# Attention weights split behind the exponentials and partly by transfers; a fifth pair of hidden tiles and another order of norms in the first feed-forward stage

## The chip, the cores and the metric

The kernel runs on one core of one Trainium2 chip. The metric is the device time of one execution, in microseconds. The kernel before takes 1312.35 us (median of three runs, 1311.97 to 1312.97).

Engines: PE (TensorE) multiplies matrices, DVE (VectorE) and ACT (ScalarE) work element by element and move matmul results from PSUM to SBUF, POOL (GpSimd) does small vector work and issues some DMAs, SP (SyncE) issues most DMAs.

## The reference, cut to what matters

A trunk of two layers over 512 tokens of width 1024: a Mamba-2 layer, then attention with a compressed key and value, each followed by a feed-forward network and by layer norms of a weighted residual.

```python
def trunk(x):
    mix = ssd_mixer(x, ...)
    h = layer_norm(DN_ALPHA * x + mix, ln_mix_g[0], ln_mix_b[0])
    h = layer_norm(DN_ALPHA * h + conv_ffn(h, ...), ln_ffn_g[0], ln_ffn_b[0])
    k_nope, k_rope, v = mla_shared_kv(h, ...)
    mix = mla_attention(h, ..., k_nope, k_rope, v)
    h = layer_norm(DN_ALPHA * h + mix, ln_mix_g[1], ln_mix_b[1])
    return layer_norm(DN_ALPHA * h + conv_ffn(h, ...), ln_ffn_g[1], ln_ffn_b[1])

def conv_ffn(h, up, conv_w, conv_b, down):
    u = causal_depthwise_conv(h @ up, conv_w, conv_b)
    g, val = jnp.split(u, 2, axis=-1)
    return (jax.nn.silu(g) * val) @ down

def attend(h):
    q = rms_norm(h @ q_down) @ q_up
    scores = q_nope @ k_nope.T + q_rope @ k_rope.T
    return softmax(where(causal, scores * scale, -inf)) @ v
```

The feed-forward network has 2816 hidden channels, 22 tiles of 128. Attention has 8 heads of 128, with 64 more rotary dimensions.

## The kernel before, in words

All matmuls run in a reduced-precision form of float32, and each operand is split into a high and a low half so that three matmuls (high by high, high by low, low by high) give back the precision. The activations' halves are made when a result leaves PSUM: ACT writes the high half as a cast, DVE subtracts it from the result and writes the low half. Weights go through `WStream`. It loads them in order into staging tiles `wst`, and `_split` (L76) makes two tiles of each: ACT casts `wh` (L96), DVE subtracts `wl` (L97). Six such pairs of buffers exist; `ahead(i, most)` splits as far as they and its bound allow, and `retire` gives a pair back after its last matmul.

The order of each engine's instructions is fixed when the program is built. A scheduler follows the order of the code with its own priorities, and `tc.issue_after` holds work back behind a named instruction. SP's loads are in the order of `load` calls.

The feed-forward stage (`ffn`, L420) works channel tile by channel tile: two weights, gate and value, with 24 matmuls each (`mm_a`, L159), then convolution, gate and product on ACT and DVE (`finish`). The down projection uses a form in which two hidden tiles (a pair) and two halves of the output share seven products in place of eight; `down_pairs` (L361) runs the products a11, s1, s2 with s4, s3, a12, a22 on the banks X, Y and Z. RP0 and RP1 (L288) give the pairs of each round, in parts of two or one that share a weight tile. In the first feed-forward stage the first round has five pairs (tiles 0 to 9), the second four (10 to 17); tiles 18 to 21 are plain. Sums of weight tiles that the pairs need are gathered in `rs` by loads on POOL's queue that add to what stands there (L52). After the rounds, the last part (L526) runs over the four token tiles: the plain tiles' down product, `piece`, in two halves of 12 matmuls, then `add_mix` (L185) to the residual with its sum, mean (L189), squares (L194, on ACT), variance and reciprocal deviation (L203, L204, on POOL), and the norm itself in `ln_a` (L210) and `ln_b` (L215). `transpose_h` (L267) then transposes the tile on PE and writes both halves of `ht`, which the next stage multiplies.

Attention (`mla`) begins with `down(i)` for the four token tiles, 48 matmuls each against six weights dw0 to dw5, each followed by `down_t` on the tile before. The transposes of tiles 0 and 1 stand inside the last part of the feed-forward stage, those of 2 and 3 behind down(0) and down(1). The head loop (L1352) then runs, for head h: the queries and keys of head h+1 (`qk`, evicted as qT and kT in L1235 and L1236; `qk_rope` for every second head), the value product of head h-1 (`pv`, evicted as oT in L1307 and L1308), the transposes of head h's probabilities (`ptrans`, L1288), and the scores of head h+1 (`scores`: matmul L1265, mask, maximum, exponential L1277 on ACT, scaling L1279 on DVE into E). Two calls of `ws.ahead(n[0], most=1)` per head split one weight each: hw1 to hw7 (640 wide, one per head) and the output weights ow0 to ow7 (1024 wide).

## Time and profile before

| | |
|---|---|
| median of three runs | 1312.35 us (1311.97 to 1312.97) |
| the profiled execution | 1311.7 us |
| its span | 1310.0 us |
| PE busy | 1299.5 us (99%) |
| DVE busy | 1020.6 us (78%) |
| ACT busy | 636.0 us (49%) |
| POOL busy | 93.1 us (7%) |
| mean granted PE clock | 0.998 of full speed, the 2.4 GHz level |

The span is the time from the first to the last instruction; the execution's own time has 1.7 us around it. Busy time is the time in which an engine has an instruction under way. A group of matmuls in the chain of work overlaps from one to the next, so the length of a group over its count gives the pitch of one, and the duration of a single matmul is longer than that.

### The profile page before, as it was taken

How to read it: one execution, taken by the hardware profiler on the slowest of the kernel's cores; microseconds unless marked ns; L12 is line 12 of the kernel's file. 1: busy time of each engine (PE TensorE's matmuls, PEld its weight loads, DVE VectorE, ACT ScalarE, POOL GpSimd, SP SyncE). 2: the span in 40 equal slices, each digit the busy share in tenths (PEclk: the TensorE clock that was granted, in tenths of full speed). 3: DMA queues.
4: the chain of work that ended last, by engine and by line, in shares of the span. 5: the costliest groups of instructions: out<-in, count | busy, mean ns of one | idle time of the engine just before them, and what ended most of it. 6: DMA issues, size and time to landing. Idle time of an engine off the chain costs nothing.

```text
span 1310.0 us, 17422 instructions
## 1 busy us (share of the span) xinstructions
PE 1299.5 (99%) x6666; PEld 1098.9 (84%) x6666; DVE 1020.6 (78%) x1581; ACT 636.0 (49%) x1029; POOL 93.1 (7%) x96
## 2 busy tenths in 40 slices
PE   9999999999999999999999999999999999999997
PEld 8888888888888988888888899888898888888886
DVE  7888888797798868866766876898587686667587
ACT  6765555455453544444443434665254444444341
POOL 0111011011011001100000012000100010000000
PEclk9999999999999999999999999999999999999999
DMA  8423322313410433352311822121144227323251
GB/s 297 179 113 129 113 88 90 132 58 133 161 65 10 171 129 81 80 207 98 123 58 31 254 81 62 71 107 49 35 149 135 79 35 213 130 97 105 41 161 65
DMA packets 49779, 144.59 MB, mean 110 GB/s; under 512 B 5312, under 2 KB 6336, under 8 KB 48416
## 3 DMA queue, kind: packets, MB, share of 16 engines
q1 hardware_dynamic: 44480, 133.57, 28.8%
q0 software_dynamic: 5072, 9.77, 4.4%
q8 instruction: 52, 0.85, 0.3%
q14 instruction: 31, 0.25, 0.1%
q10 hardware_dynamic: 144, 0.15, 0.0%
HBM read 141.30 MB, written 2.16 MB: 110 GB/s over the span
## 4 chain that ended last, share of the span: by engine, by line
PE 95%; DVE 4%; ACT 1%; issue 0%; DVEq 0%; ACTq 0%
PE ps L159 57%; PE ps L165 10%; PE ps L167 10%; PE ps L166 10%; PE ps L803 1%; PE ps L915 1%; PE ps L811 1%; PE ps L274 1%; PE ps L792 1%; PE ps L742 1%; PE ps L1265 1%; DVE wl L97 1%; DVE PT L1291 1%; PE ps L770 1%; DVE E L1279 0%; DVE smx L1275 0%
## 5 line engine op out<-in xcount | busy, mean ns | idle before, releaser
L159 PE MATMUL ps<-ht,wh 128*128 128x512 f32 (+1 forms) x2256 | 517.0, 379 | 0.0
L159 PEld LDWEIGHTS ps<-ht,wh 128*128 128x128 f32 x2256 | 408.1, 188 | 79.7 <-issue 1.4
L97 DVE TENSOR_TENSOR wl<-wst,wh 128x1024 fp32r<-128x1024 f32 (+3 forms) x222 | 256.3, 1169 | 44.2 <-ACT wh L96 43.3
L96 ACT CAST wh<-wst 128x1024 fp32r<-128x1024 f32 (+3 forms) x222 | 218.8, 995 | 114.3 <-PE ps L167 62.3
L159 PE MATMUL ps<-ht,wl 128*128 128x512 f32 (+1 forms) x1128 | 266.6, 378 | 0.0
L159 PEld LDWEIGHTS ps<-ht,wl 128*128 128x128 f32 x1128 | 205.2, 188 | 39.6
L328 DVE SCALAR_TENSOR_TENSOR acc<-ps,cw,acc 128x511 f32<-128x511 f32 x88 | 65.7, 747 | 80.0 <-ACT acc L327 80.0
L165 PE MATMUL ps<-wh,gt 128*128 128x512 f32 (+1 forms) x320 | 123.7, 387 | 0.0
L167 PE MATMUL ps<-wh,gt 128*128 128x512 f32 (+1 forms) x320 | 123.6, 386 | 0.0
L166 PE MATMUL ps<-wl,gt 128*128 128x512 f32 (+1 forms) x320 | 123.6, 386 | 0.0
L340 ACT CAST gt<-acc 128x512 fp32r<-128x512 f32 (+1 forms) x80 | 44.0, 571 | 102.0 <-DVE acc L333 99.3
L657 DVE SCALAR_TENSOR_TENSOR cv<-ps,cw,cv 128x511 f32<-128x511 f32 (+2 forms) x96 | 71.3, 746 | 26.8 <-ACT cv L655 25.9
L327 ACT ACTIVATE acc<-ps,cw 128x512 f32<-128x512 f32 x88 | 68.3, 776 | 29.5 <-PE ps L159 29.4
L167 PEld LDWEIGHTS ps<-wh,gt 128*128 128x128 f32 x320 | 60.1, 188 | 12.3
L332 ACT ACTIVATE acc<-acc 128x512 f32<-128x512 f32 x44 | 27.8, 632 | 87.6 <-DVE acc L329 87.5
L165 PEld LDWEIGHTS ps<-wh,gt 128*128 128x128 f32 x320 | 60.1, 188 | 12.1
L166 PEld LDWEIGHTS ps<-wl,gt 128*128 128x128 f32 x320 | 60.1, 188 | 12.1
L329 DVE SCALAR_TENSOR_TENSOR acc<-ps,cw,acc 128x510 f32<-128x510 f32 x88 | 65.8, 748 | 2.5
L52 POOL DMA_DIRECT2D rs<-in_down_dram x24 | 25.4, 1058 | 572.7 <-DVE wl L97 572.7
L96 ACT CAST wh<-rs 128x1024 fp32r<-128x1024 f32 (+1 forms) x48 | 39.9, 834 | 46.4 <-DVE rs L88 27.1
L341 DVE TENSOR_TENSOR gt<-acc,gt 128x512 fp32r<-128x512 f32 (+1 forms) x80 | 48.8, 627 | 13.5 <-ACT gt L340 13.5
L387 DVE SCALAR_TENSOR_TENSOR h<-h,ps 128x512 f32<-128x512 f32 x56 | 37.6, 686 | 26.0 <-PE ps L167 26.0
(242 smaller groups left out, 1744.7 us busy)
## 6 DMA issues: line engine op xcount, KB each, us to landing
wst<-in_up_dram SPq DMA_DIRECT2D x88, 512.0 KB, 3.5
wst<-in_xbc_dram SPq DMA_DIRECT2D x32, 512.0 KB, 6.0
wst<-in_down_dram SPq DMA_DIRECT2D x26, 512.0 KB, 5.5
W<-cumd SPq DMA_DIRECT2D x8, 1024.0 KB, 4.6
wst<-in_sow_dram SPq DMA_DIRECT2D x16, 512.0 KB, 3.6
wst<-in_zw_dram SPq DMA_DIRECT2D x14, 512.0 KB, 6.1
rs<-in_down_dram POOLq DMA_DIRECT2D x12, 512.0 KB, 6.9
wst<-in_down_dram SPq DMA_DIRECT2D x18, 256.0 KB, 2.6
```

The lines of the kernel that those rows point to most:

```text
L96: nc.scalar.copy(h[:, :f], s[:, :f])
L97: nc.vector.tensor_tensor(l[:, :f], s[:, :f], h[:, :f], op=ALU.subtract)
L159: nc.tensor.matmul(out, w[:, k, :], xts[k][:, x, ts], start=first and p == 0 and k == 0, stop=last and p == 2 and k == nk - 1, skip_group_ ...
L165: nc.tensor.matmul(out, xt[:, 0, tsl], wh, start=start, stop=False, skip_group_check=True)
L166: nc.tensor.matmul(out, xt[:, 0, tsl], wl, start=False, stop=False, skip_group_check=True)
L167: nc.tensor.matmul(out, xt[:, 1, tsl], wh, start=False, stop=stop, skip_group_check=True)
L327: nc.scalar.activation(a, b, AF.Identity, bias=cw[:, ch, 3:4], scale=cw[:, ch, 2:3])
L328: nc.vector.scalar_tensor_tensor(a[:, 1:], b[:, :SEQ - 1], cw[:, ch, 1:2], a[:, 1:], op0=ALU.mult, op1=ALU.add)
L329: nc.vector.scalar_tensor_tensor(a[:, 2:], b[:, :SEQ - 2], cw[:, ch, 0:1], a[:, 2:], op0=ALU.mult, op1=ALU.add)
L340: k.nc.scalar.copy(dst[:, 0, :], src)
L341: k.nc.vector.tensor_tensor(dst[:, 1, :], src, dst[:, 0, :], op=ALU.subtract)
L657: nc.vector.scalar_tensor_tensor(t[:, d:], b[:, :SEQ - d], cw[:, ch, 3 - d:4 - d], t[:, d:], op0=ALU.mult, op1=ALU.add)
```

## The change

In `_split` a new kind "d" makes the low half without DVE: ACT writes the negative of the weight, rounded, into `wl`, and a DMA on POOL's queue adds the staged weight to it. Seventeen weights have this kind: dw0 to dw5, hw1 to hw7 and ow0 to ow3. In the head loop one call for up to two weights, behind the last exponential and scaling of the next head's scores, stands in place of the two calls for one each.

In the first feed-forward stage the second round has five pairs, tiles 10 to 19. Tiles 20 and 21, the plain ones, are computed behind the first product a11 (`late`); the banks Y and Z are taken later, and the norm's parameters are loaded behind s2 and s4. The last part has 6 matmuls per half tile in place of 12. Its loop is written out anew for this stage: tile 0 is transposed behind tile 2's second half, tile 1's squares and norm come behind that, and tiles 1, 2 and 3 are transposed inside down(0), down(1) and down(2), after 33 of 48 matmuls (MID).

```diff
@@ WStream._split
         nc.scalar.copy(h[:, :f], s[:, :f])
-        nc.vector.tensor_tensor(l[:, :f], s[:, :f], h[:, :f], op=ALU.subtract)
+        if kind == "d":
+            nc.scalar.activation(l[:, :f], s[:, :f], AF.Copy, scale=-1.0)
+            nc.gpsimd.dma_start(l[:, :f], s[:, :f], accum_op=ALU.add)
+        else:
+            nc.vector.tensor_tensor(l[:, :f], s[:, :f], h[:, :f], op=ALU.subtract)
@@ rounds
-RP0 = ((2, 2, 1), (2, 1, 1))
+RP0 = ((2, 2, 1), (2, 2, 1))
+NGT = 18
...
-    return r0, r0 + 2 * sum(rp[1])
+    r1 = r0 + 2 * sum(rp[1])
+    return r0, r1, min(HT, r1 + NGT - 3 * sum(rp[1]) - (sum(rp[1]) + 1) // 2)
@@ down_pairs
         product(X, "a11", p, n + p, True, True)
     n += ni
     ahead(n, add(X, 0, 0, 1))
+    n = late(n)
+    Y = new_banks()
     for p in range(ni):
         product(Y, "s1", p, n + p, True, True)
     n += ni
     ahead(n, add(Y, 1, 1, 1))
-    between()
     for p in range(ni):
         product(X, "s2", p, n + 2 * p, False, True)
         product(Y, "s4", p, n + 2 * p + 1, False, True)
     n += 2 * ni
+    between()
+    Z = new_banks()
@@ ffn, the last part of the first stage
+            for i in range(NT):
+                added = half(i, 0)
+                if i == 1:
+                    with tc.issue_after(added.ins):
+                        ln_b(0, 0)
+                        ln_b(0, 1)
+                half(i, 1)
+                if i == NT - 1:
+                    ws.ahead(n + 2 * nw, la)
+                if i == 2:
+                    a, d = k.transpose_h(0)
+                    with tc.issue_after(a.ins), tc.issue_after(d.ins):
+                        squares(1)
+                        norm_a(1)
+                        for f in range(2):
+                            ln_b(1, f)
+                k.ln_mean(i)
+                if i != 1:
+                    squares(i)
+                    norm_a(i)
+                if i == NT - 1:
+                    for j in (2, NT - 1):
+                        for f in range(2):
+                            ln_b(j, f)
...
-        k.pend = [lambda: k.transpose_h(NT - 2), lambda: k.transpose_h(NT - 1)]
+        k.pend = [lambda i=i: k.transpose_h(i) for i in range(1, NT)]
@@ mla
+                if mid and c == MID:
+                    mid()
...
-            down(i)
-            if k.pend:
-                k.pend.pop(0)()
+            down(i, k.pend.pop(0) if k.pend else None)
@@ mla, the head loop
-                ends = qk(h + 1)
-                a, d = qk_rope(h + 1) or ends
-                with tc.issue_after(a.ins), tc.issue_after(d.ins):
-                    ws.ahead(n[0], most=1)
+                qk(h + 1)
+                qk_rope(h + 1)
...
-            a, d = ptrans(h)
+            ptrans(h)
             if h + 1 < AH:
+
+                a, d = scores(h + 1)
                 with tc.issue_after(a.ins), tc.issue_after(d.ins):
-                    ws.ahead(n[0], most=1)
-            if h + 1 < AH:
-                scores(h + 1)
+                    ws.ahead(n[0], most=2)
```

ACT in the head loop, from an exponential of the second head's scores to the value product's oT. In the kernel before, E is the exponentials (L1277), qT and kT the evictions of the third head's queries and keys, PT the transposed probabilities (L1290), wh the cast of a weight:

```order
L1277 ACTIVATE E_7515,smx<-ps,smx 128x128
L1277 ACTIVATE E_7528,smx<-ps,smx 128x256
L1235 ACTIVATE qT<-ps 128x512
L1277 ACTIVATE E_7541,smx<-ps,smx 128x384
L1235 ACTIVATE kT<-ps 128x512
L1277 ACTIVATE E_7554,smx<-ps,smx 128x512
L96 CAST wh<-wst 128x1024
L1307 CAST oT<-ps 128x512
L1290 CAST PT_7608<-ps 128x512
```

In the changed kernel the same stretch, where the exponential is L1326, the eviction L1286, the transposed probabilities L1340 and the weight's halves L97 and L99:

```order
L1326 ACTIVATE E_7508,smx<-ps,smx 128x128
L1326 ACTIVATE E_7521,smx<-ps,smx 128x256
L1286 ACTIVATE qT<-ps 128x512
L1326 ACTIVATE E_7534,smx<-ps,smx 128x384
L1326 ACTIVATE E_7547,smx<-ps,smx 128x512
L97 CAST wh<-wst 128x640
L99 ACTIVATE wl<-wst 128x640
L97 CAST wh<-wst 128x640
L99 ACTIVATE wl<-wst 128x640
L1286 ACTIVATE kT<-ps 128x512
L1356 CAST oT<-ps 128x512
L1340 CAST PT_7609<-ps 128x512
```

Before, kT's eviction stands ahead of the last exponential and one cast behind it; now two weights of two instructions each stand between the last exponential and kT.

DVE in the last part of the first feed-forward stage, from tile 2's second sum to the transposes of tile 1. In the kernel before (L185 is a sum, L210 and L215 the norm, L278 a transposed low half, L97 a weight's low half):

```order
L185 SCALAR_TENSOR_TENSOR h,lnst<-h,ps 128x512
L189 TENSOR_SCALAR lnst<-lnst 128x1
L210 SCALAR_TENSOR_TENSOR xn<-h,lnst,lng 128x512
L278 TENSOR_TENSOR ht<-ps,ht 128x4x128 x2
L210 SCALAR_TENSOR_TENSOR xn<-h,lnst,lng 128x512
L97 TENSOR_TENSOR wl<-wst,wh 128x1024
L185 SCALAR_TENSOR_TENSOR h,lnst<-h,ps 128x512
L215 SCALAR_TENSOR_TENSOR h<-xn,lnst,lnb 128x512 x2
L97 TENSOR_TENSOR wl<-wst,wh 128x1024
L97 TENSOR_TENSOR wl<-wst,wh 128x768 x2
L185 SCALAR_TENSOR_TENSOR h,lnst<-h,ps 128x512
L278 TENSOR_TENSOR ht<-ps,ht 128x4x128 x2
```

In the changed kernel (L190 a sum, L194 a mean, L215 and L220 the norm, L283 a transposed low half):

```order
L194 TENSOR_SCALAR lnst<-lnst 128x1
L283 TENSOR_TENSOR ht<-ps,ht 128x4x128 x2
L215 SCALAR_TENSOR_TENSOR xn<-h,lnst,lng 128x512 x2
L220 SCALAR_TENSOR_TENSOR h<-xn,lnst,lnb 128x512 x2
L215 SCALAR_TENSOR_TENSOR xn<-h,lnst,lng 128x512 x2
L190 SCALAR_TENSOR_TENSOR h,lnst<-h,ps 128x512 x2
L220 SCALAR_TENSOR_TENSOR h<-xn,lnst,lnb 128x512
L194 TENSOR_SCALAR lnst<-lnst 128x1
L220 SCALAR_TENSOR_TENSOR h<-xn,lnst,lnb 128x512
L215 SCALAR_TENSOR_TENSOR xn<-h,lnst,lng 128x512 x2
L220 SCALAR_TENSOR_TENSOR h<-xn,lnst,lnb 128x512 x2
L283 TENSOR_TENSOR ht<-ps,ht 128x4x128 x2
```

The weights' low halves are gone from this stretch, and tile 1's transposed low halves stand behind the norm of tile 3, where they stood ahead of it.

PE around the transposes of tile 1. In the kernel before (L274; the matmuls ahead are the last part's, those behind it down(0)'s):

```order
L165 MATMUL ps<-wh,gt 128x512
L166 MATMUL ps<-wl,gt 128x512
L167 MATMUL ps<-wh,gt 128x512
L274 MATMUL ps<-ident,h 128x128 x8
L165 MATMUL ps<-wh,ht 128x384
L166 MATMUL ps<-wl,ht 128x384
L167 MATMUL ps<-wh,ht 128x384
```

In the changed kernel (L279), inside down(0):

```order
L172 MATMUL ps<-wh,ht 128x384
L170 MATMUL ps<-wh,ht 128x320
L171 MATMUL ps<-wl,ht 128x320
L172 MATMUL ps<-wh,ht 128x320
L279 MATMUL ps<-ident,h 128x128 x8
L170 MATMUL ps<-wh,ht 128x320
L171 MATMUL ps<-wl,ht 128x320
L172 MATMUL ps<-wh,ht 128x320
```

The transposes have moved from the end of the last part to 33 matmuls into down(0).

## Rows read from the trace of the kernel before

**Rows 1.** The page, its first and its fourth part: busy time of each engine, its share of the span and its instructions; then the shares of the chain of work that ended last, by engine.
```profile
PE 1299.5 (99%) x6666; PEld 1098.9 (84%) x6666; DVE 1020.6 (78%) x1581; ACT 636.0 (49%) x1029; POOL 93.1 (7%) x96
...
PE 95%; DVE 4%; ACT 1%; issue 0%; DVEq 0%; ACTq 0%
```

**Rows 2.** The view of waits, for PE: line of the matmul, releaser and its line; microseconds in total, number of times, the longest. L1265 is the score matmuls of a head, L1288 the transposes of its probabilities.
```profile
PE ps L1288 <- DVE E L1279: 1.0, 2, 0.7
...
PE ps L1265 <- DVE oT L1308: 0.8, 3, 0.3
...
PE ps L1265 <- DVE kT L1236: 0.2, 1, 0.2
```

**Rows 3.** The timeline of PE in attention: start and duration in us, engine, line, operation, output and inputs, shape, count; in brackets the idle time before it and its releaser. A matmul's duration overlaps the next one's start.
```profile
857.29 0.44 PE L1288 MATMUL ps<-ident,E 128*128 128x128 f32 x2 [0.65 <-DVE E L1279]
...
869.60 0.33 PE L1265 MATMUL ps<-ka,qrT 128*128 128x384 f32 x1
...
869.78 0.34 PE L1265 MATMUL ps<-kb,qrT 128*128 128x384 f32 x1
...
870.37 0.50 PE L1265 MATMUL ps<-kT,qT 128*128 128x512 f32 x1 [0.25 <-DVE oT L1308]
```

**Rows 4.** Stretches of the span: start and end, length, then busy time and instructions of PE, weight loads, DVE, ACT and POOL, the granted clock of PE as a share, the share of time with transfers, GB/s. They are: the first round of the first feed-forward stage; the products of its second round; its last part with the next stage's first transposes; the first of the four `down` of the attention stage; seven and a half of attention's heads.
```profile
430.04:579.09 149.05, 149.05 (x715) 125.87 (x715) 115.14 (x165) 70.61 (x94) 7.29 (x8) 1.00 0.41 121
...
709.65:747.57 37.92, 37.92 (x169) 31.38 (x168) 30.86 (x40) 18.02 (x23) 2.99 (x3) 1.00 0.58 185
...
747.57:771.02 23.45, 23.45 (x113) 19.58 (x112) 20.43 (x38) 9.14 (x13) 2.67 (x6) 1.00 0.29 92
...
771.02:778.81 7.79, 7.79 (x52) 7.76 (x51) 6.93 (x12) 2.51 (x5) 0.74 (x2) 1.00 0.57 192
...
837.00:907.50 70.50, 68.62 (x405) 60.38 (x404) 67.22 (x178) 46.37 (x119) 0.00 (x0) 1.00 0.25 90
```

**Rows 5.** The chain of work, for two groups: start, length, engine, line, count of matmuls. L159 are 512-wide; L274 is the eight 128-wide transposes of one tile.
```profile
84.18 21.79 PE ps L159 x96
...
778.97 0.87 PE ps L274 x8
```

**Rows 6.** The timeline in attention, DVE and, in the last row, POOL: weight splits (L97), and POOL's addition in the rotary step (L1119).
```profile
848.60 0.83 DVE L97 TENSOR_TENSOR wl<-wst,wh 128x640 fp32r<-128x640 f32 x1
...
868.37 1.23 DVE L97 TENSOR_TENSOR wl<-wst,wh 128x1024 fp32r<-128x1024 f32 x1 [0.24 <-ACT wh L96]
...
822.88 2.64 DVE L97 TENSOR_TENSOR wl<-wst,wh 128x640 fp32r<-128x640 f32 x2
...
823.04 1.80 POOL L1119 TENSOR_TENSOR qr<-qr,rtmp 128x512 f32<-128x512 f32 x1 [5.52 <-DVE qr L1118]
```

**Rows 7.** The timeline of ACT in attention: weight casts (L96), the end of the last exponential of a score row (L1277) and the eviction of kT (L1235).
```profile
847.64 0.71 ACT L96 CAST wh<-wst 128x640 fp32r<-128x640 f32 x1
...
864.53 0.21 ACT L1277 ACTIVATION_READ_ACCUMULATOR E<-ps,smx 128x1 f32 x1
...
864.69 0.60 ACT L1235 ACTIVATE kT<-ps 128x512 fp32r<-128x512 f32 x1
...
867.30 1.03 ACT L96 CAST wh<-wst 128x1024 fp32r<-128x1024 f32 x1
```

**Rows 8.** The timeline of the last part of the first feed-forward stage: on DVE the addition of the product to the residual with its sum (L185), the mean (L189), the two steps of the norm (L210, L215), a tile's transposed low halves (L278); on ACT the sum of squares (L194), a tile's transposed high halves (L277) and a 768-wide weight cast (L96); on POOL the power that gives the reciprocal deviation (L204).
```profile
751.78 0.68 DVE L185 SCALAR_TENSOR_TENSOR h<-h,ps 128x512 f32<-128x512 f32 x1
...
753.94 0.21 DVE L189 TENSOR_SCALAR lnst<-lnst 128x1 f32<-128x1 f32 x1
...
754.19 1.42 DVE L210 SCALAR_TENSOR_TENSOR xn<-h,lnst,lng 128x512 f32<-128x512 f32 x2
...
756.54 1.41 DVE L215 SCALAR_TENSOR_TENSOR h<-xn,lnst,lnb 128x512 f32<-128x512 f32 x2
...
765.75 1.28 DVE L278 TENSOR_TENSOR ht<-ps,ht 128x512 fp32r<-128x512 f32 x2
...
754.25 1.15 ACT L194 ACTIVATE lnjunk<-h,lnst 128x1024 bf16<-128x1024 f32 x1 [5.42 <-DVE lnst L189]
...
764.53 1.08 ACT L277 CAST ht<-ps 128x512 fp32r<-128x512 f32 x2 [3.60 <-PE ps L274]
...
769.11 0.84 ACT L96 CAST wh<-wst 128x768 fp32r<-128x768 f32 x1 [0.30 <-PE ps L167]
...
755.86 0.57 POOL L204 TENSOR_TENSOR lnst<-lnst,mhalf 128x1 f32<-128x1 f32 x1
```

**Rows 9.** DMA issues in two stretches, 684 to 700 us (the first two rows) and 719 to 734 us (the next four): output and source, queue, count, KB each, median us from issue to landing. The rs rows on POOL's queue add what they load to what stands in SBUF. The last row is the timeline of POOL: the issue of one of them.
```profile
rs<-in_down_dram POOLq DMA_DIRECT2D x1, 512.0 KB, 5.8
...
rs<-in_down_dram POOLq DMA_DIRECT2D x2, 256.0 KB, 4.0
...
rs<-in_down_dram POOLq DMA_DIRECT2D x1, 512.0 KB, 7.8
...
rs<-in_down_dram POOLq DMA_DIRECT2D x2, 256.0 KB, 8.1
...
lng<-in_gb_dram SPq DMA_DIRECT2D x1, 512.0 KB, 7.7
...
lnb<-in_gb_dram SPq DMA_DIRECT2D x1, 512.0 KB, 9.4
...
685.10 1.20 POOL L52 DMA_DIRECT2D rs<-in_down_dram  x1 [133.74 <-DVE wl L97]
```

More of the change, by code (lines that the diff above doesn't have):

```diff
@@ L314, in ffn_items @@
                 j += 2 * n
+            if r and kinds == "r":
+                it += ups(range(RL, HT))
     for hf in range(2):
@@ L358, in pair_operands, with down_pairs @@
     split(k, s34, v)
-def down_pairs(k, ws, n, prs, parts, first, between):
+def down_pairs(k, ws, n, prs, parts, first, late, between):
     nc = k.nc
-    X, Y, Z = ([k.bank() for _ in range(2)] for _ in range(3))
+    new_banks = lambda: [k.bank() for _ in range(2)]
+    X = new_banks()
     ni = len(parts)
@@ L487, in ffn, with channels @@
                 c0 += 2
-            for ci in range(c0, HT if r else R0):
-                bg, bv = k.bank(), k.bank()
-                ws.ahead(n + 1)
-                for b, i in ((bg, n), (bv, n + 1)):
-                    w = [x.rearrange("p (k m) -> p k m", k=KT) for x in ws.get(i)]
-                    k.mm_a(b, w, k.ht, slice(0, 512))
-                    ws.retire(i)
-                n += 2
-                ws.ahead(n)
-                finish(ci, bg, bv)
+            def channels(cs, n):
+                for ci in cs:
+                    bg, bv = k.bank(), k.bank()
+                    ws.ahead(n + 1)
+                    for b, i in ((bg, n), (bv, n + 1)):
+                        w = [x.rearrange("p (k m) -> p k m", k=KT) for x in ws.get(i)]
+                        k.mm_a(b, w, k.ht, slice(0, 512))
+                        ws.retire(i)
+                    n += 2
+                    ws.ahead(n)
+                    finish(ci, bg, bv)
+                return n
+            n = channels(range(c0, RL if r else R0), n)
             if mid and not r:
                 mid()
-            n = down_pairs(k, ws, n, prs, rp[r], not r, norm_params if r else lambda: None)
+            late = lambda n: channels(range(RL, HT), n) if r else n
+            n = down_pairs(k, ws, n, prs, rp[r], not r, late, norm_params if r else lambda: None)
         if out is None:
@@ L523, in ln_b, with half, norm_a, squares @@
                 nc.sync.dma_start(out[i * P:(i + 1) * P, fs], k.h[:, i, fs])
-        for i in range(NT):
+        def half(i, f):
+            b = k.bank()
+            piece(i, b, f, 0, 512, i == NT - 1)
+            return k.add_mix(i, f, b, 1.0, True)
+        def norm_a(i):
+            xn[i] = row("xn")
+            k.ln_a(i, xn[i])
+        def squares(i):
+            k.ln_squares(i)
+            k.ln_var(i, nc.gpsimd)
+        if out is None:
+            for i in range(NT):
[22 more added lines that the diff above has]
+                            ln_b(j, f)
+        for i in range(0 if out is None else NT):
             last = i == NT - 1
@@ L533, in ffn @@
                     ln_b(i - 1, 0)
-                    if out is None or not last:
+                    if not last:
                         ln_b(i - 1, 1)
-            if out is not None and last:
+            if last:
                 bs = [k.bank(), k.bank()]
@@ L541, in ffn @@
                 continue
-            b = k.bank()
-            piece(i, b, 1, 0, 512, last)
-            if last:
-                ws.ahead(n + 2 * nw, la)
-            k.add_mix(i, 1, b, 1.0, True)
-            if out is None and i >= 2:
-                k.transpose_h(i - 2)
-            xn[i] = row("xn")
-            k.ln_stats(i)
-            if out is None:
-                k.ln_var(i, nc.gpsimd)
-            k.ln_a(i, xn[i])
-            if out is not None:
-                k.ln_var(i, nc.vector)
-        if out is None:
-            for f in range(2):
-                ln_b(NT - 1, f)
+            half(i, 1)
+            k.ln_stats(i)
+            norm_a(i)
+            k.ln_var(i, nc.vector)
         n += 2 * nw
@@ L574 @@
 DRAM = bass.MemoryType.DRAM
+MID = 11
 def ssd_items(xbc, zdt, zw, ow):
@@ L1065, in mla_items @@
 def mla_items(dw, vw, rw, hw, ow):
-    it = [(dw[j], 1024) for j in range(4)] + [(dw[j][:, :768], 768) for j in (4, 5)]
+    it = [(dw[j], 1024, "d") for j in range(4)] + [(dw[j][:, :768], 768, "d") for j in (4, 5)]
     rv = rw.rearrange("(k p) n -> p k n", p=P)
@@ L1071, in mla_items @@
     it += [(vv[:, :, hf * 512:(hf + 1) * 512], 1024) for hf in range(2)]
-    it += [(hw[h], 640) for h in range(AH)]
-    it += [(ow[j * P:(j + 1) * P, :], 1024) for j in range(AH)]
+    it += [(hw[h], 640) + ("d",) * (h > 0) for h in range(AH)]
+    it += [(ow[j * P:(j + 1) * P, :], 1024) + ("d",) * (j < 4) for j in range(AH)]
     return it
@@ L1142, in mla, with down @@
         tok = {}
-        def down(i):
+        def down(i, mid):
             bq, bk = k.bank(), k.bank()
@@ L1240, in qk @@
                 n[0] += 1
-            return a, d
         def qk_rope(h):
```

42 lines of the change are left out of this document (20 added, 22 removed).

## The prediction

> **What bounds the kernel now.** The page first [rows 1]: TensorE (PE) is busy 1299.5 of 1310.0 us and makes 95% of the chain that ended last, VectorE (DVE) 4%, ScalarE (ACT) 1%. So time goes only by fewer matmuls or by closing PE's gaps. The view of waits, for PE [rows 2], tells where gaps are: the E tiles, oT and kT, all attention, 2.0 us together. Matmul starts give more, since a restarted pipeline also loses its overlap. In PE's timeline [rows 3] two 384-wide matmuls of a score row start 0.18 apart (869.60 and 869.78), the next only 0.59 later (870.37): 0.41 lost where the row names 0.25. Five other places look alike, 857.29 the longest; by starts I make it about 3.2 us, all of it between 837 and 907.
>
> The table by stretches [rows 4] says which engine is close behind. In the first feed-forward stage and its last part PE's busy time equals the stretch; DVE has 7 us to spare in 709.65:747.57 and 3.0 in 747.57:771.02. In attention DVE is busy 67.22 of 70.50 us and ACT 46.37. So DVE sets the gaps there, and ACT has room on average.
>
> The profiled execution took 1311.7 us, 0.65 under the median of 1312.35. The sum below is a difference; I put it on the median.
>
> **1. The fifth pair: -1.4 us.** Two plain channels and their down rows cost 48 matmuls in the last stage (two per weight half, four tiles, three products); in a pair they cost 7 products x 2 halves of 3 = 42. Hence 6 fewer. One 512-wide matmul costs 21.79 / 96 = 0.227 us [rows 5]: 6 x 0.227 = 1.36. The extra pair adds DVE and ACT work on operands and 512-wide weight sums; the first round of the same stage already runs five pairs with products straight behind its channels, and PE there is busy 149.05 of 149.05 us [rows 4]. Channels 20 and 21 now stand behind the first product, which gives their 96 matmuls (21.8 us) as cover for the weights of the second. The wait on Y and Z banks is later than before by their late allocation, not earlier. The rs loads pass two up loads on SP and the norm parameters go behind s2 and s4; three products of 30 matmuls (20.4 us) still separate them from their use, while such loads landed in 7.7 and 9.4 us [rows 9]. Cost 0; if cover were gone, a load that late would cost at most its overshoot, under 1 us.
>
> **2. Attention: -0.7 us.** What leaves DVE: the low halves of seven 640-wide and four 1024-wide weights (0.83 and 1.22 us each [rows 6]), some 10.7 of its 67.22 us. The gap on E (857.29 [rows 3]) comes of a DVE that is late with the last E; with splits out of its queue most of 1.0 goes. The gap on oT at 870.37 stands behind the split at 868.37, which oT's low half follows: such gaps shrink too. What comes: ACT makes both halves. Its order in heads 2 and 3 is now four 640-wide instructions between the last exponential and kT's eviction. A 640-wide cast takes 0.71, a 1024-wide one 1.03, kT's eviction 0.60 [rows 7]. Before, kT stood ahead of the last exponential or followed it at once (864.53 to 864.69). In head 3 kT is late by 4 x 0.7 = 2.8 us. PE at this place still has the previous head's values and the transposes, about 1.5 us, so I charge 1.25. Head 2 has its kT behind q-rope matmuls: 0.5. The 1024-wide pair (2.06 us) in heads 4 to 7 has most of that cover: 0.2 twice. The gap at 837 (0.37) stays. New gaps 0.37 + 0.5 + 1.25 + 0.4 = 2.5 against 3.2, so -0.7. Ends: all but 837's gap gone, -2.8; or the whole 2.8 us uncovered in head 3 beside 0.5, 0.4 and 0.37, which is 4.1 and +0.9. The DMAs that add the staged weight here have a head (10 us) and more to land.
>
> **3. Norms and the down products behind them: +0.9 us.** Zero is PE's start on tile 0 in the last stage. Eight pieces of 6 matmuls end at 10.9 us, transposes (0.87 [rows 5]) at 11.8, down(0) with tile 1's transposes inside it at 11.8 + 7.79 + 0.87 = 20.4; 7.79 is the stretch of one down [rows 4]. At 20.8 down(1) wants the low half of tile 1. On DVE that half is last in a long queue. Tile 0's sums end at 2.72 + 0.69 = 3.4. Then come four means (0.21), four pairs of L215 (1.42), four of L220 (1.41), six sums (0.65 each), tile 0's low halves (1.28) and half of tile 1's (0.64): 0.84 + 5.7 + 5.6 + 3.9 + 1.3 + 0.6 = 18.0 [rows 8], so 21.4 without any idle time. Mean to reciprocal deviation takes 2.5 us through ACT and POOL (753.94 to 756.43: 0.21, 1.15 and 0.57 with hand-overs [rows 8]), and tile 3's stands directly ahead of the transposes: up to 1 us of idle time. So 21.4 to 22.5, a gap of 0.6 to 1.7; I take 0.9. Before, tile 1's transposes were done ahead of down(0), and DVE had its gaps later.
>
> A second latecomer lies under the same gap: weight dw5. ACT casts tile 0 from 9.0 (1.08), sums the squares of tiles 1 and 2 until 12.2 (1.05 each beside one another), then makes four 768-wide halves of 0.84 [rows 8]: dw4's by 13.9, dw5's by 15.5. PE needs their low halves at 19.5 and 18.4. Then POOL issues a transfer that adds. No transfer within SBUF is in the trace; the nearest rows are the accumulating loads from memory: 4.0 us for 256 KB and 5.8 for 512 when nothing else moves, 8.1 and 7.8 beside other loads [rows 9]. 384 KB alone is 4.9 by interpolation: dw5 at 20.4, dw4 at 18.8, both inside the gap DVE makes. Beside other loads, 7.8 up to 8.1 with an issue of 1.2 in front: 23.3 to 24.8, a gap of 3.8 to 5.3. I take the quiet row, since the stretch 747.57:771.02 has transfers for 0.29 of its time. The lower end is the transfer in time and DVE without idle time, 0.2.
>
> The Trainium skill (DMA: Bandwidth & Descriptors, "Anatomy of one DMA") gives about 2.0 us plus bytes over 436 GB/s for such a transfer; by it 384 KB takes an estimated 2.9 and dw5 is in time. The rows here, 4.0 and 5.8, are slower for their sizes, so the sum does not use it.
>
> **Sum.** -1.36 - 0.7 + 0.9 = -1.15: 1312.35 - 1.15 = 1311.2 us (profiled execution about 1310.5).
>
> **Rivals.** A: *late adds.* POOL writes the transfers' descriptors late or the transfers meet the weight loads; dw5 (and dw4) come at 23.3 to 24.8 and PE stands in down(0). For it: the loads beside others in [rows 9], and the 640-wide pair of L97 that took 2.64 us instead of 1.66 while POOL ran L1119, which itself took 1.80 [rows 6]: the two engines do slow each other. Against it: a POOL issue amid DVE's splits took 1.2 us [rows 9]. Time: 1312.35 - 2.06 + 3.8 to 5.3 = 1314.1 to 1315.6, take 1314.9. It makes the kernel slower once dw5 lands more than 2.1 us after 19.5. The Trainium skill (SBUF — State Buffer, "SBUF: two separate sides") says transfers queued by GpSimd starve for descriptors while VectorE runs some two-port operations; that is this rival, and the row at 823.04 [rows 6] is the only one that leans its way.
>
> B: *attention clears.* ACT has 24 us of slack over 70, and the split hides behind the value products; only 837's gap and 0.3 remain (-2.5), and the norm gap is 0.2. -1.36 - 2.5 + 0.2 = -3.7: 1308.7. For it: DVE is the engine near the bound, and loses a sixth of its work. Against it: kT's place in ACT's order.
>
> C: *ACT becomes the bound in heads.* kT late in several heads, attention +0.9 instead of -0.7: 1312.35 - 1.36 + 0.9 + 0.9 = 1312.8. Also what it comes to if the moved pair work costs PE its 1.4 us.
>
> **Chances.** Forecast 0.46, B 0.25, C 0.15, A 0.14. What this measurement can tell from no change is about 0.2%, 2.6 us: faster means under 1309.73, slower over 1314.97. B lies mostly below, with a little of the forecast: faster 0.26. A has its middle at the bound and C a tail: slower 0.11. The rest is 0.63. The forecast's own range is 1310.0 to 1312.4; for 8 in 10 I take in B to 1308.4 and most of A to 1315.0.
>
> **What would show it.** Right: no PE wait between the first feed-forward stage's channels and its last part; PE waits for ht's low half in down(1) by about 1 us and for no wl in down(0); in the heads the waits on oT and E fall under 0.5 together and those on kT rise to 1.5, mostly head 3. Wrong: a wait on wl from a DMA of over 2 us in down(0) (A); no kT wait in head 3 (B); kT waits in five heads or more (C); fewer than 6 matmuls gone, or PE idle time in 579 to 747.

## The result and the profile after

The changed kernel takes 1315.5 us (median of 11 runs, 1314.94 to 1316.66) against 1312.35 us before: a ratio of 1.0026, with a 95% interval of 1.0018 to 1.0033. It is slower by 3.1 us, clear of noise; forecast were 1311.2 us and a range to 1315.0. Its profiled execution took 1315.62 us.

The page of the changed kernel, busy time and the chain by engine, answers to [rows 1]:

```profile
PE 1300.7 (99%) x6660; PEld 1099.5 (84%) x6660; DVE 1008.6 (77%) x1568; ACT 651.2 (50%) x1046; POOL 109.7 (8%) x113
...
PE 95%; DVE 2%; ACT 1%; issue 1%; DMA 0%; POOL 0%; DVEq 0%; ACTq 0%; POOLq 0%
```

PE has six instructions fewer, as it should, and is no more the bound than before; the time came in as gaps. The view of PE's waits, which answers to [rows 2], shows that the old waits on E and oT are all gone and others stand there. L1314 is the scores, L171 the second of the three matmuls of a product; kT and qrT are the operands of the scores, wl a weight's low half:

```profile
PE ps L1314 <- DVE kT L1287: 1.2, 4, 0.4
...
PE ps L1314 <- ACT kT L1286: 1.1, 3, 0.6
...
PE ps L171 <- DMA wl<-wst: 1.0, 1, 1.0
...
PE ps L1314 <- DVE qrT L1302: 0.4, 2, 0.3
```

Where the time went is read best from places that both kernels have. All times are starts in the trace, in us; the second column of the changed kernel is a second profile of it.

| place | before | changed | changed, again |
|---|---|---|---|
| PE's first 512-wide matmul | 17.94 | 18.83 | 18.36 |
| first matmul of down(0) | 771.02 | 769.80 | 769.29 |
| first transpose of head 0's probabilities | 835.91 | 837.01 | 836.56 |
| first transpose behind the attention output | 934.52 | 937.72 | 937.22 |
| PE's last matmul | 1302.17 | 1305.37 | 1304.87 |
| end of the span | 1310.00 | 1313.92 | 1313.69 |

The first row differs from one execution to the next (17.94 to 19.12 over all profiles taken, with the same code at the start), so the differences are counted from it. Counted so, the stretches repeat closely: from the first row to head 0 and through the heads, three more profiles of the kernel before, each with a few instructions that nothing waits for, agree with the column here within 0.05 us. Up to down(0) the changed kernel wins 2.1 us: 1.36 by six matmuls, 0.87 by a transposition that is done later. From there to head 0 it loses 2.3, of which 0.87 are that transposition: 1.5 us of gaps. In the heads it loses 2.1, behind them nothing, and 0.7 to 1.0 behind PE's last matmul. Sum: -1.4 + 0.1 + 1.5 + 2.1 + 0.7 = 3.0, and 3.3 in the second profile. The two stretches in the view of windows (length, then busy time of PE, weight loads, DVE, ACT and POOL), before:

```profile
771.02:835.91 64.89, 64.89 (x374) 59.81 (x373) 46.62 (x105) 29.66 (x67) 12.17 (x19) 1.00 0.23 76
835.91:934.52 98.61, 96.73 (x540) 84.06 (x539) 81.70 (x203) 52.45 (x129) 1.69 (x2) 1.00 0.21 76
```

and after:

```profile
769.80:837.01 67.21, 66.23 (x379) 60.55 (x378) 46.06 (x108) 34.53 (x75) 19.06 (x27) 1.00 0.38 101
837.01:937.72 100.71, 97.90 (x540) 84.85 (x539) 74.85 (x195) 58.32 (x137) 8.59 (x10) 1.00 0.39 109
```

In the heads DVE is busy 6.9 us less and ACT 5.9 more. DVE had been the engine next to the bound there; the change relieved it, and the stretch got longer.

**The heads.** The timeline of ACT, then DVE, then PE, where the exponentials of head 4 end and the scores of head 5 begin, shows why. L1326 is the exponential, L97 and L99 the two halves of a weight, L1286 and L1287 the high and low half of kT, L1328 the scaling into E, L1314 the scores:

```profile
877.34 0.69 ACT L1326 ACTIVATE E<-ps,smx 128x512 f32<-128x512 f32 x1
...
878.00 1.05 ACT L97 CAST wh<-wst 128x1024 fp32r<-128x1024 f32 x1
...
878.94 1.07 ACT L99 ACTIVATE wl<-wst 128x1024 fp32r<-128x1024 f32 x1
...
879.89 0.60 ACT L1286 ACTIVATE kT<-ps 128x512 fp32r<-128x512 f32 x1
...
878.35 0.49 DVE L1328 TENSOR_SCALAR E<-E,smx 128x512 f32<-128x512 f32 x1
...
880.52 0.69 DVE L1287 SCALAR_TENSOR_TENSOR kT<-ps,kT 128x512 fp32r<-128x512 f32 x1 [1.69 <-ACT kT L1286]
...
881.27 0.44 PE L1314 MATMUL ps<-kT,qT 128*128 128x128 f32 x2 [0.40 <-DVE kT L1287]
```

The two halves of the weight fill ACT from 878.00 to 879.89. Only then does it evict kT, for which DVE has been idle 1.69 us, and PE's scores wait for DVE's half. All of PE's gaps between 837 and 902 follow kT or the rotary operand: by matmul starts 0.4 at 838, 0.7 in head 2, 1.2 in head 3, 0.3, 1.0, 0.3 and 1.0 in heads 4 to 7, about 5 us against 3.

**The down products.** ACT, POOL, PE and DVE, where L99 is dw5's negated half, L100 the issue of dw4's and dw5's transfers, L171 the matmul that wants dw5's low half, L220 and L283 tile 3's norm and tile 1's transposed low halves:

```profile
772.26 0.85 ACT L99 ACTIVATE wl<-wst 128x768 fp32r<-128x768 f32 x1
...
772.55 1.80 POOL L100 DMA_DIRECT2D wl<-wst  x2
...
778.73 0.44 PE L171 MATMUL ps<-wl,ht 128*128 128x384 f32 x1 [0.98 <-DMA wl<-wst]
...
778.23 1.42 DVE L220 SCALAR_TENSOR_TENSOR h<-xn,lnst,lnb 128x512 f32<-128x512 f32 x2 [0.73 <-POOL lnst L209]
...
779.56 1.28 DVE L283 TENSOR_TENSOR ht<-ps,ht 128x512 fp32r<-128x512 f32 x2
```

ACT is done with dw5 at 773.1, POOL issues both transfers from 772.55 to 774.35, dw5's lands at 778.69, and PE goes on at 778.73. Tile 1's low half comes right behind, its first part at about 780.2, where PE loses 0.1 us more. Without the wait on dw5 PE would have come to that place about 1.1 us earlier and stood there until the same time: the two waits cover each other.

### The profile page after: what moved, and what is told of

It reads as the page before. It is cut to its first block, busy times and chain, and to the rows that moved or that the text cites. A ratio compares the mean times of both kernels' runs of the same rounds, so it can differ in the third digit from the quotient of the medians.

```text
span 1313.9 us, 17448 instructions
## 1 busy us (share of the span) xinstructions
PE 1300.7 (99%) x6660; PEld 1099.5 (84%) x6660; DVE 1008.6 (77%) x1568; ACT 651.2 (50%) x1046; POOL 109.7 (8%) x113
## 4 chain that ended last, share of the span: by engine, by line
PE 95%; DVE 2%; ACT 1%; issue 1%; DMA 0%; POOL 0%; DVEq 0%; ACTq 0%; POOLq 0%
PE ps L164 57%; PE ps L170 10%; PE ps L171 10%; PE ps L172 10%; PE ps L854 1%; PE ps L966 1%; PE ps L1314 1%; PE ps L862 1%; PE ps L279 1%; PE ps L843 1%; PE ps L793 1%; PE ps L821 1%; DVE PT L1341 0%; ACT E L1326 0%; PE ps L1351 0%
## 5 line engine op out<-in xcount | busy, mean ns | idle before, releaser
L97 ACT CAST wh<-wst 128x1024 fp32r<-128x1024 f32 (+4 forms) x220 | 217.8, 1001 | 110.7 <-PE ps L172 62.4
L102 DVE TENSOR_TENSOR wl<-wst,wh 128x1024 fp32r<-128x1024 f32 (+3 forms) x203 | 237.4, 1184 | 42.4 <-ACT wh L97 40.1
L171 PE MATMUL ps<-wl,gt 128*128 128x512 f32 (+1 forms) x318 | 122.9, 386 | 0.0
L171 PEld LDWEIGHTS ps<-wl,gt 128*128 128x128 f32 x318 | 59.7, 188 | 12.1
L97 ACT CAST wh<-rs 128x1024 fp32r<-128x1024 f32 (+1 forms) x48 | 41.8, 871 | 53.7 <-DVE rs L89 25.3
```

Source lines behind the costliest of these rows:

```text
L97: nc.scalar.copy(h[:, :f], s[:, :f])
L102: nc.vector.tensor_tensor(l[:, :f], s[:, :f], h[:, :f], op=ALU.subtract)
L171: nc.tensor.matmul(out, xt[:, 0, tsl], wl, start=False, stop=False, skip_group_check=True)
```

## The experiments

Each was timed beside the kernel before (1312.2 to 1312.4 us in those runs).

**The attention part undone.** The head loop and the kinds of hw and ow as before; the rest as changed.

```diff
-                qk(h + 1)
-                qk_rope(h + 1)
+                ends = qk(h + 1)
+                a, d = qk_rope(h + 1) or ends
+                with tc.issue_after(a.ins), tc.issue_after(d.ins):
+                    ws.ahead(n[0], most=1)
...
-            ptrans(h)
+            a, d = ptrans(h)
             if h + 1 < AH:
-
-                a, d = scores(h + 1)
                 with tc.issue_after(a.ins), tc.issue_after(d.ins):
-                    ws.ahead(n[0], most=2)
+                    ws.ahead(n[0], most=1)
+                scores(h + 1)
...
-    it += [(hw[h], 640) + ("d",) * (h > 0) for h in range(AH)]
-    it += [(ow[j * P:(j + 1) * P, :], 1024) + ("d",) * (j < 4) for j in range(AH)]
+    it += [(hw[h], 640) for h in range(AH)]
+    it += [(ow[j * P:(j + 1) * P, :], 1024) for j in range(AH)]
```

> The changed kernel with the attention part undone: the two splitting calls per head at their old places, hw and ow low halves by DVE again. Theory: the changed kernel lost about 2.1 us between the first and the last head (PE waits on kT, 5.1 us of gaps against 3.2), so this gives 1312.5 to 1313.5, with the old gaps on E and oT back and kT's down to 0.4. What then remains over 1312.35 is the wait in down(0) for dw5 (1.1 us) and tile 1's low half, less the pair's 1.4. Rival (the loss is of the program as a whole, as PE's first 512-wide matmul 0.9 us later and a longer tail suggest): 1314.3 or more.

Measured: 1312.59 us, ratio 1.0001 (0.9993 to 1.0010). The heads took 98.58 us as before (98.61), PE's waits on E and oT were back at 0.9 and 0.7, and the end was 7.9 us. So the attention part costs all of the loss, 2.1 us in the heads and the rest at the end; the feed-forward part by itself is worth nothing, 1.4 won and 1.5 given back.

**Only the place undone**: the part of that diff in the head loop without the kinds of hw and ow, ACT and the transfers still making the low halves.

> The changed kernel with only the place of the splits undone: two calls of one weight per head, behind the evictions of qT and kT and behind those of the probabilities; ACT and the transfers still make the low halves. Theory (the place, ahead of kT in ACT's queue, makes the loss): kT waits fall from 2.3 us to under 0.6 and the time to 1312.8 to 1313.6; as DVE is rid of the subtractions, the old waits on E and oT stay small, so it may go below the run with the whole attention part undone. Rival (ACT's extra work or the transfers make the loss, wherever they stand): 1315 or more, with PE waits on oT or the probabilities written by ACT in place of kT's.

Measured: 1314.32 us. The kT waits fell to 0.2, but PE now waited 1.9 us on oT. PE's waits and two rows of ACT's timeline:

```profile
PE ps L1316 <- DVE oT L1360: 1.9, 2, 1.0
...
PE ps L1316 <- DVE kT L1287: 0.2, 1, 0.2
...
868.76 1.06 ACT L99 ACTIVATE wl<-wst 128x1024 fp32r<-128x1024 f32 x1
...
869.85 0.59 ACT L1359 CAST oT<-ps 128x512 fp32r<-128x512 f32 x1
```

Neither theory fits alone. The place decides which eviction is late, but two instructions of 1.0 us stand ahead of one at either place. The heads cost 0.9 us instead of 2.1; the end was long here too, 8.7 us.

**Only the maker undone**: splits behind the exponentials, DVE subtracting.

```diff
-    it += [(hw[h], 640) + ("d",) * (h > 0) for h in range(AH)]
-    it += [(ow[j * P:(j + 1) * P, :], 1024) + ("d",) * (j < 4) for j in range(AH)]
+    it += [(hw[h], 640) for h in range(AH)]
+    it += [(ow[j * P:(j + 1) * P, :], 1024) for j in range(AH)]
```

> The changed kernel with hw and ow low halves by DVE, but the splits still behind the exponentials. ACT then has 1.4 us in place of 2.8 ahead of kT in head 3 and 1.0 in place of 2.1 in heads 4 to 7. Theory (ACT's queue ahead of kT): the kT gaps shrink by half or more, but DVE's subtraction stands ahead of kT's low half: 1314.0 to 1315.0. Rival (transfers slow the heads): 1313.4 or less, as the transfers are gone.

Measured: 1312.42 us, the rival's number. ACT, then DVE, at the same place as above:

```profile
876.50 1.06 ACT L97 CAST wh<-wst 128x1024 fp32r<-128x1024 f32 x1
...
877.43 0.62 ACT L1286 ACTIVATE kT<-ps 128x512 fp32r<-128x512 f32 x1
...
877.59 1.23 DVE L102 TENSOR_TENSOR wl<-wst,wh 128x1024 fp32r<-128x1024 f32 x1 [0.25 <-ACT wh L97]
...
878.73 0.68 DVE L1287 SCALAR_TENSOR_TENSOR kT<-ps,kT 128x512 fp32r<-128x512 f32 x1
```

ACT's part ahead of kT halves, and DVE's half of kT starts 1.3 us behind ACT's instead of 0.6. PE still waits on kT (1.9 us in all), as the theory says, but the old waits on E and oT are away, and the heads come out even with before. My 1314 left that gain out. The new place alone is neither gain nor loss. What costs is the second ACT instruction in front of the evictions; the transfers are gone here as well, but ACT's instructions take as long with them as without (1.05 to 1.07 us), and the runs below that make hw by transfer lose nothing in the heads.

**dw4 and dw5 by DVE.**

```diff
-    it = [(dw[j], 1024, "d") for j in range(4)] + [(dw[j][:, :768], 768, "d") for j in (4, 5)]
+    it = [(dw[j], 1024, "d") for j in range(4)] + [(dw[j][:, :768], 768) for j in (4, 5)]
```

> The changed kernel with the low halves of dw4 and dw5 by DVE, 2 x 0.84 us, ahead of tile 1's transposed low halves in DVE's queue. Theory: the 1.1 us wait on dw5's transfer goes, and DVE's queue makes tile 1's low half about 1.5 us late in its place: 1315.3 to 1316.0. Rival (DVE has idle time there that takes the two in): 1314.4.

Measured: 1315.33 us, as the theory says and no better than the changed kernel. The wait on wl is gone and this one is there:

```profile
PE ps L172 <- DVE ht L283: 1.7, 1, 1.7
```

**ACT's halves of dw4 and dw5 ahead of tile 2's squares**, on top of the first experiment.

```diff
                 if i == NT - 1:
                     ws.ahead(n + 2 * nw, la)
+                    with tc.issue_after(ws.wl4.ins):
+                        squares(2)
...
-                    squares(i)
+                    if i != 2:
+                        squares(i)
```

> The run with the attention part undone, and in ACT's queue the two halves of dw4 and dw5 ahead of tile 2's sum of squares in place of behind it. Theory: PE's 1.1 us wait in down(0) is on dw5's transfer, which starts when ACT is done with it; ACT is about 1 us earlier with it here, and tile 2's deviation, 1.2 us later, still comes before DVE wants it. Wait on wl under 0.4 us, and 1311.6 to 1312.0 in place of 1312.59. Rival (the wait is on how long the transfer takes beside other loads, or tile 1's low half stands right behind it): 1312.4 or more.

Measured: 1312.93 us, so the theory fell. Counted from PE's start on tile 0, the transfers were issued 1.1 and 1.7 us earlier, dw5's landed 0.9 later, and PE waited longer on wl, 1.7 us in all. The view of DMAs, 768 to 774.9 us, of the changed kernel (queue, count, KB each, median us to landing):

```profile
wl<-wst POOLq DMA_DIRECT2D x2, 384.0 KB, 4.6
...
wst<-in_vw_dram SPq DMA_DIRECT2D x1, 512.0 KB, 3.7
```

and of this run:

```profile
wl<-wst POOLq DMA_DIRECT2D x2, 384.0 KB, 7.1
...
wst<-in_vw_dram SPq DMA_DIRECT2D x1, 512.0 KB, 5.2
```

The transfers went out amid the loads of vw and took 7.1 us instead of 4.6.

**The loads of vw held behind dw5's transfer**, by a load of one column that has to wait for it; vw has the kind "s" and dw5 the mark "z". The rest is as in the run before.

```diff
+            if kind in ("s",) and self.held:
+                break
...
+        if part == "z":
+            nc.sync.dma_start(s[:, :1], self.items[i][0][:, :1])
+            self.held = False
```

> The run with dw4 and dw5 ahead of tile 2's squares (1312.93 us), and the loads of the next weights, vw, on SP behind a load of one column of dw5, which waits for dw5's transfer; the rest as there. In that run the two transfers were issued 1.2 to 1.8 us earlier than in the changed kernel but took 6.9 and 7.3 us in place of 3.9 and 5.3, with vw's two loads of 512 KB issued from 766 to 771. Theory (the transfers share the DMA engines with these loads): they take 4 to 5.5 us, PE's waits on wl fall from 1.7 us to under 0.3, and the time to 1311.0 to 1311.8. Rival (they are slow for the transfer of dw3 ahead of them, or for DVE): waits on wl over 0.8 us, 1312.4 or more.

Measured: 1312.57 us. The transfers took 3.9 and 4.4 us, and no wait on wl was left:

```profile
wl<-wst POOLq DMA_DIRECT2D x2, 384.0 KB, 4.1
```

That the loads make them slow is shown. The time is not as expected, for PE now waited 1.2 us on tile 1's low half, which had been hidden behind the other wait:

```profile
779.90 0.44 PE L178 MATMUL ps<-wh,ht 128*128 128x384 f32 x1 [1.20 <-DVE ht L289]
```

Where tile 2's squares stand makes no difference to it. Counted from PE's start on tile 0, DVE had the first part of that half done at 22.2 us in this run, in the run before it, in the changed kernel and with the attention part undone.

**dw0 to dw5 by DVE**, on top of the first experiment: the "d" goes from all six.

> The run with the attention part undone, and dw0 to dw5 by DVE again: only the fifth pair, with its order of norms and transposes, is left of the change. Theory: DVE's queue ahead of tile 1's low half gets 6.5 us longer, less 1.5 us of idle time in it and the 1.1 us wait on dw5 that goes; dw0 and dw1 partly ahead of it: 1314.5 to 1316.5, with a wait on ht of 3 us or more in down(1). Rival (DVE has the room): 1311.5.

Measured: 1315.60 us, with 3.2 us of waits on DVE. One of them I had not expected: tile 0's norm (L220) is late for its transposes already:

```profile
PE ps L172 <- DVE ht L283: 1.8, 1, 1.8
...
PE ps L279 <- DVE h L220: 1.4, 1, 1.4
```

So five pairs and this order of norms cost 3.3 us if DVE makes the low halves; the transfers of dw0 to dw5 save 3.0 of them.

**hw by transfer at the old places**, on top of the run with dw4 and dw5 first: hw1 to hw7 have the "d" again.

> As the run before it, and hw1 to hw7 made by ACT and a transfer, at the old places (one behind the evictions of qT and kT, one behind the probabilities); ow by DVE. With all of them by transfer at these places PE reached head 3 0.4 us earlier than with DVE and lost 1.3 us in the later heads, where the wide ones stood ahead of oT's eviction. Theory: only the first gain is left, 0.3 to 0.5 us under the run before it, 1311.2 to 1311.6. Rival (the end of the program or POOL's issues take it back): as the run before it or above.

Measured: 1312.43 us, not the 1311.2 to 1311.6 expected. In the heads it won the 0.5 us expected; the waits on dw5's transfer (0.6) and on tile 1's low half (0.2) stayed.

**The same with dw5's low half by DVE behind tile 3's mean**, tile 2's squares at the changed kernel's place.

```diff
-                    ws.ahead(n + 2 * nw, la)
+                    ws.ahead(n + 2 * nw, la, most=1)
...
-                k.ln_mean(i)
+                mean = k.ln_mean(i)
+                if i == NT - 1:
+                    with tc.issue_after(mean.ins):
+                        ws.ahead(n + 2 * nw, la)
...
-    it = [(dw[j], 1024, "d") for j in range(4)] + [(dw[j][:, :768], 768, "d") for j in (4, 5)]
+    it = [(dw[j], 1024, "d") for j in range(4)] + [(dw[4][:, :768], 768, "d"), (dw[5][:, :768], 768)]
```

> The attention part undone but for hw1 to hw7 by ACT and transfer at the old places; dw5's low half by DVE, behind tile 3's mean, where DVE waited 0.7 us for tile 3's deviation; tile 2's squares at the place of the changed kernel. Theory (late in down(0) is what the second of two transfers beside the next stage's loads costs): one transfer, dw4's, lands by 776.5 and delays PE by under 0.3 us; dw5's half takes DVE's idle time, so that tile 1's low half comes at most 0.2 us later. PE's gaps in down(0) and down(1) fall from 1.3 to 0.5 us together and the time to 1311.3 to 1311.9. Rival (DVE's 0.84 us goes fully onto the way to tile 1's low half): 1312.3 or more.

Measured: 1311.47 us, ratio 0.9993 (0.9984 to 1.0003). PE's waits are the smallest of all runs, none on wl:

```profile
PE ps L1319 <- DVE oT L1363: 0.9, 3, 0.4
...
PE ps L172 <- DVE ht L283: 0.5, 1, 0.5
...
PE ps L1343 <- DVE E L1333: 0.3, 1, 0.3
...
PE ps L1319 <- DVE kT L1290: 0.2, 1, 0.2
```

The stretches behind them, which answer to those above:

```profile
769.29:835.77 66.48, 66.02 (x379) 60.63 (x378) 46.96 (x109) 33.78 (x74) 18.04 (x26) 1.00 0.35 96
835.77:933.93 98.16, 96.82 (x539) 84.05 (x538) 78.91 (x199) 55.08 (x133) 5.13 (x6) 1.00 0.30 90
```

It beats the changed kernel by 4.0 us and has a median 0.9 under the kernel before. The interval does not settle that, though ten of its eleven runs lie under 1311.94, the fastest of the 27 runs of the kernel before beside them.

Tile 1's low half came no earlier here, 22.3 us behind PE's start on tile 0: dw5's half took the idle time of DVE, as expected. PE waited less on it because the scheduler, given this edit, put six of tile 2's eight transposes ahead of that place, where all eight stood 5 us behind it before:

```profile
778.56 0.81 PE L279 MATMUL ps<-ident,h 128*128 128x128 f32 x6
...
779.84 0.59 PE L172 MATMUL ps<-wh,ht 128*128 128x384 f32 x2 [0.46 <-DVE ht L283]
```

The wait is 0.7 us shorter than with vw held, and six of eight transposes that take 0.87 us together are 0.65.

**The end.** Its length, from the start of PE's last matmul, was 8.55 us in the changed kernel, 8.74 with only the place undone and 8.21 with dw4 and dw5 by DVE; in all other profiles but the second one of the changed kernel (below) 7.82 to 7.90. These three also have a packet more on the queue q14, which the page lists as instructions, the changed kernel's page first, then that of before:

```profile
q14 instruction: 32, 0.26, 0.1%
```

```profile
q14 instruction: 31, 0.25, 0.1%
```

In the changed kernel this packet goes out 5.7 us behind PE's last matmul, amid the last stores. They are issued where they were before, the last at 4.8 us, and land later, the last at 7.2 instead of 6.6, which is 0.6 of the 0.7 us. Their rows, changed kernel first, then before:

```profile
out_dram<-h SPq DMA_DIRECT2D x2, 128.0 KB, 2.5
```

```profile
out_dram<-h SPq DMA_DIRECT2D x2, 128.0 KB, 1.9
```

With only the place undone it is the same (packet at 5.0, last store at 7.4). That the packet slows the stores is not shown; with dw4 and dw5 by DVE the stores land at 6.6 and the packet goes out 0.5 us behind the last instruction, so the end is longer there for something else.

Four runs looked for what brings the packet about, each the kernel before with one loop more (14 and 40 times on ACT, 24 on POOL, 20 transfers). The scheduler put all of these from 714 us on, into the first feed-forward stage and not the second.

```diff
+                for _ in range(14):
+                    nc.scalar.copy(pad[:, 1:2], pad[:, 0:1])
...
+                    nc.gpsimd.tensor_scalar(pad[:, 1:2], pad[:, 0:1], 1.0, None, op0=ALU.mult)
...
+                    nc.gpsimd.dma_start(pad[:, 1:2], pad[:, 0:1], accum_op=ALU.add)
```

More instructions on ACT:

> The kernel before with 14 copies of one element more on ACT in the second feed-forward stage, where PE never waits for ACT. Three profiled kernels with more ACT and POOL instructions than the others had an end, from PE's last matmul to the end of the span, of 8.2 to 8.7 us in place of 7.8 to 7.9, and an instruction fetch on queue q14 beside the last stores. Theory (an instruction more than a fetched block on ACT): the end grows to 8.2 or more and the time to 1312.8 to 1313.2. Rival (it is POOL's instructions, or chance): 7.8 and 1312.35.

> The kernel before with 40 copies of one element more on ACT in place of 14, 1069 instructions there. The three profiled kernels with a longer end (8.2 to 8.7 us from PE's last matmul) and a 32nd packet on queue q14 have 1044 and 1046 instructions on ACT; all those with the short end have 1043 or fewer, the one with 14 copies just 1043; on POOL the number was passed without effect (120). Theory (the packet is a fetch of ACT's instructions that the end of the program waits for): 32 packets, an end of 8.2 us or more, a time of 1312.7 to 1313.1. Rival (it hangs on the transfers, or is chance): 31 packets, 7.8 us and 1312.35.

Measured: 1312.20 and 1312.01 us, 31 packets, an end of 7.8 us. More on POOL:

> The kernel before with 24 multiplications of one element more on POOL in the second feed-forward stage, which nothing waits for: as many instructions on POOL as the changed kernel has and some more. Theory (the end of the span grows by an instruction fetch of POOL; 14 more on ACT left it at 7.84 us): q14 has one packet more, the end from PE's last matmul is 8.2 us or more, the time 1312.7 to 1313.1. Rival (chance, or the transfers themselves): 7.8 us and 1312.35.

Measured: 1312.37 us, 31 packets, 7.8 us. More transfers:

> The kernel before with 20 transfers of one element a partition more on POOL's queue, from SBUF to SBUF and adding, in the second feed-forward stage; nothing waits for them. Theory (the longer end, 8.2 to 8.7 us from PE's last matmul in place of 7.8, comes with the number of transfers on POOL's queue: the three kernels that have it issue 15 or 17 more than the kernel before, those with 13 or fewer don't have it): an end of 8.2 us or more, a 32nd packet on q14, 1312.7 to 1313.3. Rival (chance in single profiles): 7.8 to 7.9 us, 31 packets and 1312.3.

Measured: 31 packets and an end of 7.9 us; the number of transfers alone does not do it. Its time, 1326.2 us, is of another cause: the scheduler put the 20 transfers ahead of the norms on POOL, one waiting for the other, and PE waited for tile 0:

```profile
PE ps L274 <- DVE h L215: 11.9, 1, 11.9
```

The changed kernel once more:

> The changed kernel once more, for a second profile of it: if its long end is its own, the end is again 8.2 us or more, q14 has 32 packets; the start of PE's 512-wide matmuls, 17.9 us in the profile of before and 18.2 to 19.1 in all the others, is of the single execution. PE's gaps should be as in the first profile: about 2.1 us more than before in the heads and 1.4 us in down(0) and down(1); 1315.5 us.

Measured: 1315.41 us, 32 packets, an end of 8.82 us (packet at 5.0, last store at 7.5), 2.1 us lost in the heads and 1.5 in the down products. The waits on wl are two here, dw4's and dw5's, 1.0 us together as in the first profile. The long end belongs to the kernel, and what makes it stays open.

## Why the prediction was wrong

Of the 4.3 us between the forecast and the measurement, the stretches put 2.8 on attention, 0.6 on the norms and down products and 0.7 on the end.

**Step 1, the fifth pair (-1.36)** held: down(0) starts 2.1 us earlier, of which 0.87 are the transposition, and no wait stands between the stage's channels and its last part.

**Step 2, attention (-0.7)** failed, at +2.1. The step that failed is the charge for heads 4 to 7: "The 1024-wide pair (2.06 us) in heads 4 to 7 has most of that cover: 0.2 twice." They cost 0.3, 1.0, 0.3 and 1.0, together 2.6 in place of 0.4. The parts beside it were right: head 3 at 1.2 (1.25 forecast), head 2 at 0.7 (0.5), 0.4 at the first, the waits on E and oT gone. The mechanism was right and the cover was not looked up: from the last exponential of head 4 on, PE has 3.1 us of value products and transposes (877.2 to 880.3), and both halves of kT are there after 3.9 (877.3 to 881.2); where rotary transposes stand there as well, the gap is 0.3. Head 3's charge, taken from the same chain, should have been carried to each later head: the prediction's own 1.5 us of cover, for which it shows no row, leaves 0.6 of the 2.06 in each of four heads. Rival C named this mechanism and priced it at +0.9; it kept the idea of cover too. The six old gaps come to 2.9 us by starts, not 3.2, which makes another 0.3 of the miss.

**Step 3, norms and down products (+0.9)** had the mechanism right and the size too small, at 1.5. The places came out well: dw5 was wanted 19.6 us behind PE's start on tile 0 (758.0) and landed at 20.7 (19.5 and 20.4 forecast), tile 1's low half came at 22.2 (21.4 to 22.5). The transfer's wait lay inside the gap that DVE makes, as forecast: by starts PE lost 1.1 us on dw5 and 0.1 on the low half, the rest of the 1.5 in pieces of 0.1 or less, and with vw held 1.4 on the low half alone. What was mis-sized is DVE's way to that half: 22.2 is 0.8 past the 21.4 without idle time, where a gap of 0.9 had room for 0.3; the wait for tile 3's deviation alone, in the rows above, is 0.73. (In the sentence on dw4's and dw5's halves the prediction has the two places, 19.5 and 18.4, in the wrong order; its sum uses 19.5 for dw5, which is right.)

Rival A's mechanism was half true: the transfers collide with loads, and in the changed kernel they happened to start when the loads were nearly through. That 1315.5 lies in A's range, 1314.1 to 1315.6, is luck: A has PE wait 3.8 to 5.3 us on dw5, where it lost 1.1, and wins in attention, where the loss was. A transfer of 384 KB took 3.8 us alone, 4.4 to 5.5 as the second of two and 5.6 to 7.3 amid the loads, in two runs; its issue on POOL took 0.86 to 0.96 us amid DVE's norms.

The rule of the Trainium skill (DMA: Bandwidth & Descriptors, "Anatomy of one DMA"), an estimated 2.9 us for it, was too short in each case. Of the Trainium skill's descriptors that starve beside VectorE (SBUF — State Buffer, "SBUF: two separate sides") no run here shows anything.

**The end (+0.7)** stood in no step and in no rival: the prediction put it at nothing without saying so.

The range ended at 1315.0, 0.5 us short. Bounds for one head should have been multiplied by the heads that share the pattern: 2.8 in head 3 and 1.0 in each of the four later heads make attention +4.5 (0.37 + 0.5 + 2.8 + 4.0 - 3.2) and put the upper end at 1316.4.

## What to carry to other kernels

Work that is moved to an engine with spare time delays whatever stands behind it in that engine's queue; before moving it, look up which evictions come next there and who waits for them, in each turn of the loop. A transfer in place of a subtraction is worth having where its landing has slack, and that slack has to cover the loads beside it: the same 384 KB took 3.8 to 7.3 us here. When one of two waits at a place is removed, the other one is the time: here tile 1's low half came 22.2 to 22.3 us behind PE's start on tile 0 in every version but the two that gave two or more subtractions to DVE, and PE gained only where six transposes stood in front of it.

## What was not expected of the hardware

An adding transfer within SBUF of one element a partition took 2.0 us when nothing else moved and up to 7.0 beside loads (the run with 20 of them). One of 384 KB took 3.8 us alone; those of 512 KB (dw0 to dw3) took 6.3 to 10.1 beside each other and the weight loads. The end of the program was 0.4 to 1.0 us longer in the kernels with one more instruction packet on q14, and no number of instructions or transfers that was tried brought the packet about. In two of these kernels the packet went out amid the last stores, whose last one landed 0.6 to 0.9 us later than before.
